# Fifty elementwise instructions go from GpSimd to VectorE between attention and the up projection

## Chip, core and metric

The kernel runs on one core of a Trainium2 chip. The metric is the device time of one execution in microseconds (us), lower is better. Before the change the median of three runs is 1442.89 us (1441.45 to 1444.49). The execution that was profiled took 1444.43 us; its trace spans 1442.6 us.

The engines are named as in the profile: PE is TensorE (matmuls), DVE is VectorE, ACT is ScalarE, POOL is GpSimd, and SP only issues DMAs here. Each engine works through its own queue strictly in order; an instruction that waits holds up all behind it.

## The reference, cut to what matters

One decoder layer on x of 1024 positions by 1024 features, all in float32:

```python
h = rmsnorm(x, attn_norm_g[l]); proj = h @ w_in[l]
# two groups of eight attention heads; each group normalised, then one output projection
x = x + o @ w_out[l]
h = rmsnorm(x, ffn_norm_g[l])
u = causal_dwconv(h @ w_up[l], conv_w[l], conv_b[l])     # width 3
gate, val = jnp.split(u, 2, axis=-1)                     # 2816 columns each
x = x + (jax.nn.silu(gate) * val) @ w_down[l]
return rmsnorm(x, final_norm_g)
```

The change touches the stretch from `o @ w_out` to the first columns of `h @ w_up`.

## The kernel before, in words

**Matmuls in two parts.** Float32 operands are split into a high part (a cast, `wh`, `xh`, ...) and a low part (the value less its high part, `wl`, `xl`, ...). `mm3` (L158 to 161) does each product in three matmuls: high by high, high by low, low by high. So each weight tile needs a cast, usually on ACT, and a subtraction, on DVE or POOL, before PE can use it. In the profile a matmul of line L161 takes a `wl` or an `xl`.

**The output projection** (loop at L772) makes x2 = x + o @ w_out in 16 products: halves c = 0, 1 of the positions, and m = 0 to 7, 128 features each. DVE takes each product out of PSUM (L790, `t`), adds it to x (L791), and SP stores it (L792). ACT squares it (L800) and a running sum `sqa` is kept (L802). The weights come in tiles `w_o` of 1024 columns, two pieces each, split by `W.split` (L131): with `act=True` the cast is on ACT (L140) and the low part on POOL (L143). Eight tiles of w_out and the first three of w_up (`w_up[0..2]`, NPRE = 3) are of this kind, 22 pieces in all. During half c = 1 DVE also normalises half 0 (`normed`, L766) and takes its low parts `b11`, `b21` (L762).

**The norm of half 1.** When the last sum of squares is there, PE adds over the features (L749), DVE and ACT make the factor `rr`, PE spreads it over partitions (L184), ACT copies it to `rbc` (L758). Then the second half can be normalised (L766; for q = 3 and 7 ACT and POOL do it, L949).

**The up projection** multiplies in a seven-product scheme (Strassen and Winograd), step j = 0 to 21, with weight blocks a11, a12, a22 and sums s1 to s4 of weight blocks, and the activations `b11, b21, b22` and their sums `t1` to `t4`. For j < 3 the products with a11 and a12 are done early (`first`, `second`), from `w_up`. The loop after L944 makes t1 to t4 and b22, all on DVE, with casts on ACT. `raws(j)` loads the two raw weight tiles of a step (v and g) into two buffers that are shared by all raw weights (`wraw`, bufs=2): a load starts when everything that reads the old tile is done. `sums` and `sums2` (L879 to 887) make s1 to s4 on POOL; s1, s2 and s3 have one buffer each, and s4 lies in that of s2. `produce` casts on ACT (L905) and takes the low part (L907): s1 and s3 on DVE, the rest on POOL. The split tiles lie in three pair buffers (`wspl`), free again when PE has used them.

**What sets the order.** SP's queue stands in program order. For the other engines a scheduler sets the order when the kernel is built, so that moving an instruction to another engine can also move its neighbours.

Of the kernel before, what the change touches and what calls it, by code (L numbers as in the profile page):

```python
# [13 lines left out]
ALU = mybir.AluOpType  # L14
# [11 lines left out]
NJ = DFF // P  # L26
# [23 lines left out]
LO_UP = ("s3", "s1")  # L50
LO_FIRST = ("a11", "a22", "a12")
# [12 lines left out]
def f32(ap):  # L64
    return ap.bitcast(F32)
# [3 lines left out]
def layer(ctx, tc, xT, wqk, wv0, wv, wout, wup, wdn, cols, fbias, yT):  # L69
    nc = tc.nc  # L70
# [43 lines left out]
    class W:  # L114
# [16 lines left out]
        def split(self, upto):  # L131
            if self.done == 0 and upto > 0:
                self.dma()
                self.hi = self.pool.tile([P, self.n if self.own else 1056], F32R, name=self.tag + "h")
                self.lo = self.pool.tile([P, self.n if self.own else 1056], F32R, name=self.tag + "l")
            while self.done < upto:
                q = self.n // self.pieces
                sl = slice(self.done * q, (self.done + 1) * q)
                if self.act:
                    nc.scalar.copy(self.hi[:, sl], self.raw[:, sl])  # L140
                else:
                    nc.gpsimd.tensor_scalar(self.hi[:, sl], self.raw[:, sl], 1.0, 0.0, ALU.mult, ALU.add)  # L142
                nc.gpsimd.tensor_tensor(self.lo[:, sl], self.raw[:, sl], f32(self.hi[:, sl]), ALU.subtract)  # L143
                self.done += 1

        def get(self):
# [78 lines left out]
    rbc = const.tile([P, T], F32, name="rbc")  # L225
# [107 lines left out]
    with tc.tile_pool(name="ps_0", bufs=6, space=PSUM) as ps0, \  # L333
            tc.tile_pool(name="st0", bufs=4) as st0:
        sqa = st0.tile([P, T], F32, name="sqa", bufs=1)
# [13 lines left out]
        for k in range(KT):  # L349
# [8 lines left out]
            else:  # L358
                sq = st0.tile([P, T], F32, name="sq", bufs=2)
# [5 lines left out]
        for k in range(KT):  # L365
# [4 lines left out]
            for u in range(2):  # L370
                wh, wl = w_qk[u].get()
                for c in range(2):
                    if k == 0:
                        psq[u, c] = ps0.tile([P, 512], F32, name="p0")
                    sl = slice(c * 512, (c + 1) * 512)
# [253 lines left out]
    def out_step(part, m, c, k, ps):  # L629
        og = fill["og"]  # L630
        sl = slice(c * 512, (c + 1) * 512)
        w = w_o[part, m // 2]
        wh, wl = w.get()
        kk = (m % 2) * 4 + k
        oh, ol = og[k if part == 0 else 4 + k]
        mm3(ps, wslice(wh, kk), wslice(wl, kk), oh[:, sl], ol[:, sl], k == 0, k == 3)
        return w, sl
# [90 lines left out]
    x2 = {}  # L728

    def load_x2(m, c):  # L730
        x2[m, c] = x2p.tile([P, 512], F32, name=f"x2_{m}_{c}")
        nc.sync.dma_start(x2[m, c], x2d[m][c])
# [6 lines left out]
    def bank():  # L739
        turn[0] += 1  # L740
        if (turn[0] - 1) % 8 < 6:
            return ps_u.tile([P, 512], F32, name="u")
        return ps_p.tile([P, 512], F32, name="pj")

    def norm_cols(sqs, n):
        pn = bank()
        for tb in range(n):
            for i, sq in enumerate(sqs):
                nc.tensor.matmul(pn[:, tb:tb + 1], sq[:, tb * P:(tb + 1) * P], ones,  # L749
                                 start=(i == 0), stop=(i == len(sqs) - 1))  # L750
        rr = small.tile([P, TB], F32, name="rr")
        rsqrt_mean(rr[:, :n], pn[:, :n], n, D)
        return rr

    def norm_rows(rr, n, dst):
        pb = bank()
        spread(pb, rr, 0, n)
        nc.scalar.copy(dst, pb[:, :n * P])  # L758
# [5 lines left out]
    def normed(k, c):  # L764
        t = x2[k, c]
        nc.vector.scalar_tensor_tensor(t, t, gcol(C_GF, k), rbc[:, c * 512:(c + 1) * 512],  # L766
                                       op0=ALU.mult, op1=ALU.mult)
        return t

    sqs = {}  # L770
    for c in range(2):
        sl = slice(c * 512, (c + 1) * 512)  # L772
        for m in range(KT):
            if (m, c) not in x2:
                load_x2(m, c)
            if c == 0:
                if m + 4 < KT and (m + 4, 0) not in x2:
                    load_x2(m + 4, 0)
                if m >= 4:
                    for q in (2 * m - 8, 2 * m - 7):  # L780
                        load_x2(q, 1)
            if c == 0 and m < 2:
                ps = box[m]
            else:
                ps = bank()
                for k in range(4):
                    w, _ = out_step(1 + c, m, c, k, ps)
                    w.ahead(((m % 2) * 4 + k + 1) / 8)
            t = stg.tile([P, 512], F32, name="t1", tag="full")
            nc.vector.tensor_tensor(t, ps, rbc[:, sl], ALU.mult)  # L790
            nc.vector.tensor_tensor(x2[m, c], x2[m, c], t, ALU.add)  # L791
            nc.sync.dma_start(x2f[m][c], x2[m, c])  # L792
            if m == 0:
                if c == 1:
                    rr = norm_cols(sqs[0], 4)
                sqa = x2p.tile([P, 512], F32, name="sqa")
                act(sqa, x2[m, c], AF.Square)
            else:
                sq = stg.tile([P, 512], F32, name="sq", tag="hl")
                act(sq, x2[m, c], AF.Square)  # L800
                if m < KT - 1:
                    nc.gpsimd.tensor_tensor(sqa, sqa, sq, ALU.add)  # L802
                else:
                    sqs[c] = (sqa, sq)
            if c == 1:
                if m == 1:
                    norm_rows(rr, 4, rbc[:, :512])
                elif m > 1:
                    for k in (m - 2,) if m < 6 else (2 * m - 8, 2 * m - 7):
                        f = normed(k, 0)  # L810
                        split(b11[k] if k < 4 else b21[k - 4], f)
# [60 lines left out]
    def sums(j):  # L872
        d = st[j]
        w = steps[j][2] * P
        g, v = d["g"], d["v"]
        for n in ("s1", "s2", "s3"):
            d[n] = sp_.tile([P, 512], F32, name=n)[:, :w]
        d["s4"] = d["s2"]
        nc.gpsimd.tensor_tensor(d["s1"], v[:, :w], v[:, w:], ALU.add)  # L879
        nc.gpsimd.tensor_tensor(d["s2"], d["s1"], g[:, :w], ALU.subtract)  # L880

    def sums2(j):
        d = st[j]
        w = steps[j][2] * P
        g, v = d["g"], d["v"]
        nc.gpsimd.tensor_tensor(d["s3"], g[:, :w], v[:, :w], ALU.subtract)
        nc.gpsimd.tensor_tensor(d["s4"], g[:, w:], d["s2"], ALU.subtract)

    def pair_tile():
        return wspl.tile([P, 1056], F32R, name="wh"), wspl.tile([P, 1056], F32R, name="wl")  # L890

    def produce(i):
        j, n = stream[i]
        if i % 2 == 0:
            tiles[i // 2] = pair_tile()
        h, l = tiles[i // 2]
        w = steps[j][2] * P
        o = (i % 2) * 512
        raws(j)
        d = st[j]  # L900
        if n[0] == "s" and "s1" not in d:
            sums(j)
        src = {"a11": lambda: d["g"][:, :w], "a12": lambda: d["g"][:, w:],
               "a22": lambda: d["v"][:, w:]}.get(n, lambda: d[n])()
        nc.scalar.copy(h[:, o:o + w], src)  # L905
        eng = nc.vector if j > NJ or n in (LO_UP if j < NJ else LO_FIRST) else nc.gpsimd
        eng.tensor_tensor(l[:, o:o + w], src, f32(h[:, o:o + w]), ALU.subtract)  # L907
        made[j, n] = ((h, l), o)
        if n == "s2":
            sums2(j)  # L910
        if n == ("a12" if j >= NPRE else "a22"):
            raws(j + 1)
# [22 lines left out]
    def hi(dst, src):  # L935
        nc.scalar.copy(dst[0], src)

    def lo(dst, src):
        nc.vector.tensor_tensor(dst[1], src, f32(dst[0]), ALU.subtract)
# [5 lines left out]
    for k in range(4):  # L945
        f12, f22, f11, f21 = x2[k, 1], x2[k + 4, 1], x2[k, 0], x2[k + 4, 0]
        for q in (k, k + 4):
            if q in (3, 7):
                nc.gpsimd.tensor_tensor(x2[q, 1], x2[q, 1], rbc[:, 512:], ALU.mult)  # L949
            else:  # L950
                normed(q, 1)
        nc.vector.tensor_tensor(f11, f12, f11, ALU.subtract)
        if k:
            lo(t2[k - 1], x4[k - 1])
        if k == 2:
            x4[k] = x2p.tile([P, 512], F32, name="sqa")
        else:
            x4[k] = stg.tile([P, 512], F32, name="t2f", tag="full")
        nc.vector.tensor_tensor(x4[k], f22, f11, ALU.subtract)
        hi(t2[k], x4[k])  # L960
        nc.vector.tensor_tensor(f21, x4[k], f21, ALU.subtract)
        if k < 2:
            ahead_to(k)
        if k:
            hi(t4[k - 1], x2[k + 3, 0])
# [76 lines left out]
    for j in range(NJ):  # L1042
        d = st[j]
        for n in PORD:
# [3 lines left out]
            w, o = made[j, n]  # L1048
# [59 lines left out]
    for s in range(NJ, NS):  # L1108
        c, mp, kn = steps[s]
        ev, od_ = 2 * mp, 2 * mp + 1  # L1110
        for n in PORD:
# [5 lines left out]
            w, o = made[s, n]  # L1117
# [64 lines left out]
    for i, (t0, tn) in enumerate(PARTS):  # L1182
        h, o = t0 // 512, t0 % 512
        sqa = sp_.tile([P, 512], F32, name=f"s{i % 2 + 1}")[:, :tn]
        for m in range(KT):
# [7 lines left out]
            v = y[m, h][:, o:o + tn]  # L1193
            tt(v, ps, v, ALU.add)
            sq = stg.tile([P, T], F32, name="sq", tag="hl")[:, :tn]
# [82 lines left out]
```

## Time and profile before

| | |
|---|---|
| median of three runs | 1442.89 us |
| profiled execution, its trace's span | 1444.43 us, 1442.6 us |
| busy: PE, DVE, ACT, POOL | 1315.3, 1115.6, 620.7, 859.2 us |
| instructions: DVE, POOL | 1588, 730 |

Times in the trace are us from the start of the span. Attention ends at about 660; the output projection's halves run from 662.7 and 685; the MLP's own first operands are made from 729.6; step 1 of the up projection starts on PE at 777.5, and from 832 PE has no gap until the down projection. A granted clock of 1.00 is 2.4 GHz, 0.5 is 1.2 GHz.

In the timelines a row of several instructions (x4) gives the first start and the time up to the last end.

### The profile page before, as it was taken

How to read it: one execution, taken by the hardware profiler on the slowest of the kernel's cores; microseconds unless marked ns; L12 is line 12 of the kernel's file. 1: busy time of each engine (PE TensorE's matmuls, PEld its weight loads, DVE VectorE, ACT ScalarE, POOL GpSimd, SP SyncE). 2: the span in 40 equal slices, each digit the busy share in tenths (PEclk: the TensorE clock that was granted, in tenths of full speed). 3: DMA queues.
4: the chain of work that ended last, by engine and by line, in shares of the span. 5: the costliest groups of instructions: out<-in, count | busy, mean ns of one | idle time of the engine just before them, and what ended most of it. 6: DMA issues, size and time to landing. Idle time of an engine off the chain costs nothing.

```text
span 1442.6 us, 19157 instructions
## 1 busy us (share of the span) xinstructions
PE 1315.3 (91%) x6640; PEld 1076.8 (75%) x6640; DVE 1115.6 (77%) x1588; ACT 620.7 (43%) x1128; POOL 859.2 (60%) x730
## 2 busy tenths in 40 slices
PE   7999999999898887889788899999999988999895
PEld 5879877877787765677556688888888866878685
DVE  6246555655676677787979999998888999899987
ACT  5134434445454564353443443344334454344334
POOL 7344454444747573454657788887877774455423
PEclk9999999999999999899979999999999999999998
DMA  5556555545444455547321233333222265544313
GB/s 179 180 160 181 152 158 158 153 142 131 153 116 122 118 170 139 167 140 259 120 80 59 81 110 109 110 109 110 95 96 95 85 222 201 176 156 146 113 35 117
DMA packets 97233, 194.89 MB, mean 135 GB/s; under 512 B 8680, under 2 KB 35688, under 8 KB 97136
## 3 DMA queue, kind: packets, MB, share of 16 engines
q1 hardware_dynamic: 96272, 193.04, 42.7%
q8 instruction: 52, 0.85, 0.2%
q10 hardware_dynamic: 864, 0.64, 0.1%
q14 instruction: 45, 0.37, 0.1%
HBM read 132.79 MB, written 60.85 MB: 134 GB/s over the span
## 4 chain that ended last, share of the span: by engine, by line
PE 50%; DMA 16%; DVE 14%; POOL 9%; issue 7%; ACT 2%; SPq 2%; DVEq 0%; POOLq 0%; ACTq 0%
PE u L161 8%; PE u L160 8%; PE u L159 8%; PE pj L161 5%; PE pj L159 5%; PE pj L160 5%; DVE fbt L493 3%; DMA q<-qkd 2%; DMA vd<-vs 2%; DMA wraw<-in_wqk_dram 2%; POOL wl L907 2%; DMA wraw<-in_wv_dram 2%; PE tp L505 2%; DMA fbt<-nfd 2%; PE o L526 2%
## 5 line engine op out<-in xcount | busy, mean ns | idle before, releaser
L143 POOL TENSOR_TENSOR wl<-wraw,wh 128x256 fp32r<-128x256 f32 (+2 forms) x134 | 124.5, 947 | 29.0 <-ACT wh L140 28.7
L494 POOL TENSOR_TENSOR w<-w,fbt 128x128 f32<-128x128 f32 (+3 forms) x64 | 90.5, 1423 | 85.5 <-DVE fbt L493 56.3
L905 ACT CAST wh<-s 128x512 fp32r<-128x512 f32 (+1 forms) x136 | 79.9, 591 | 128.3 <-POOL s L880 69.5
L493 DVE TENSOR_TENSOR_SCAN fbt<-fbt 128x128 f32<-128x128 f32 (+3 forms) x64 | 103.4, 1621 | 27.9 <-ACT fbt L480 24.1
L142 POOL TENSOR_SCALAR wh<-wraw 128x256 fp32r<-128x256 f32 (+1 forms) x112 | 57.0, 526 | 110.4 <-DMA wraw<-in_wqk_dram 59.8
L879 POOL TENSOR_TENSOR s<-wraw 128x512 f32<-128x512 f32 (+1 forms) x34 | 54.9, 1613 | 95.8 <-DVE wl L907 55.0
L505 PE MATMUL tp<-ident,w 128*128 128x128 f32 x576 | 92.9, 279 | 20.6 <-DVE pl L514 10.0
L159 PE MATMUL pj<-xh,wh 128*128 128x512 f32 x224 | 101.8, 455 | 5.2 <-DVE yf L293 5.2
L907 POOL TENSOR_TENSOR wl<-wraw,wh 128x512 fp32r<-128x512 f32 x60 | 103.0, 1723 | 0.6 <-ACT wh L905 0.6
L505 PEld LDWEIGHTS tp<-ident,w 128*128 128x128 f32 x576 | 69.8, 143 | 40.1 <-DVE pl L514 13.8
L907 POOL TENSOR_TENSOR wl<-s,wh 128x512 fp32r<-128x512 f32 x48 | 87.9, 1830 | 16.6 <-ACT wh L905 14.2
L514 DVE TENSOR_TENSOR pl<-tp,ph 128x512 fp32r<-128x512 f32 x96 | 64.9, 685 | 40.2 <-ACT ph L513 39.9
L161 PE MATMUL pj<-xh,wl 128*128 128x512 f32 x224 | 90.7, 405 | 0.0
L160 PE MATMUL pj<-xl,wh 128*128 128x512 f32 x224 | 90.2, 402 | 0.0
L485 ACT ACTIVATE w<-w,m 128x128 f32<-128x128 f32 (+3 forms) x64 | 49.7, 776 | 91.8 <-DVE m L475 85.9
L1004 DVE SCALAR_TENSOR_TENSOR tg<-ua,col,tg 128x1023 f32<-128x1023 f32 (+1 forms) x44 | 88.1, 2002 | 0.0
L480 ACT ACTIVATE fbt<-s 128x512 f32<-128x512 f32 (+2 forms) x96 | 47.8, 498 | 85.6 <-PE s L470 37.4
L489 POOL TENSOR_SCALAR w<-w,l 128x128 f32<-128x128 f32 (+3 forms) x64 | 47.9, 753 | 59.1 <-DVE l L488 31.0
L905 ACT CAST wh<-wraw 128x512 fp32r<-128x512 f32 (+1 forms) x96 | 55.1, 589 | 61.7 <-DMA wraw<-in_wdn_dram 25.3
L513 ACT CAST ph<-tp 128x512 fp32r<-128x512 f32 x96 | 55.7, 590 | 54.1 <-PE o L525 35.6
L1004 DVE SCALAR_TENSOR_TENSOR tv<-ub,col,tv 128x1023 f32<-128x1023 f32 (+1 forms) x44 | 74.0, 1681 | 5.8 <-ACT tv L1002 5.7
L466 PE MATMUL s<-kh,q 128*128 128x256 f32 (+2 forms) x192 | 69.6, 365 | 9.6 <-DMA kh<-qkd 8.0
(361 smaller groups left out, 4561.2 us busy)
## 6 DMA issues: line engine op xcount, KB each, us to landing
wraw<-in_wup_dram SPq DMA_DIRECT2D x47, 512.0 KB, 3.7
st<-td SPq DMA_DIRECT2D x74, 256.0 KB, 3.9
qkd<-hl SPq DMA_DIRECT2D x32, 512.0 KB, 3.2
td<-tg SPq DMA_DIRECT2D x44, 256.0 KB, 2.3
vd<-vs SPq DMA_DIRECT2D x32, 256.0 KB, 4.5
q<-qkd SPq DMA_DIRECT2D x16, 512.0 KB
kh<-qkd SPq DMA_DIRECT2D x32, 256.0 KB, 16.6
kl<-qkd SPq DMA_DIRECT2D x32, 256.0 KB, 17.4
```

The lines of the kernel that those rows point to most:

```text
L143: nc.gpsimd.tensor_tensor(self.lo[:, sl], self.raw[:, sl], f32(self.hi[:, sl]), ALU.subtract)
L159: nc.tensor.matmul(ps, ah, bh, start=start, stop=False)
L160: nc.tensor.matmul(ps, ah, bl, start=False, stop=False)
L161: nc.tensor.matmul(ps, al, bh, start=False, stop=stop)
L466: nc.tensor.matmul(s[:, :cn], qb, kh[:, c0:c0 + cn], start=True, stop=False)
L493: nc.vector.tensor_tensor_scan(qt[:, rev], qt[:, rev], qt[:, rev], 1.0, ALU.mult, ALU.bypass)
L494: nc.gpsimd.tensor_tensor(w[:, :n], w[:, :n], qt[:, T - n + 1:T + 1], ALU.mult)
L505: nc.tensor.transpose(tp[:, a * 256 + b * P:a * 256 + (b + 1) * P], ws[2 * g + b][:, kb * P:(kb + 1) * P], ident)
L514: nc.vector.tensor_tensor(pl[:, z:], tp[:, z:], f32(ph[:, z:]), ALU.subtract)
L905: nc.scalar.copy(h[:, o:o + w], src)
L907: eng.tensor_tensor(l[:, o:o + w], src, f32(h[:, o:o + w]), ALU.subtract)
L1004: nc.vector.scalar_tensor_tensor(t[:, s:], us[:, :T - s], col[:, cw + tap:cw + tap + 1], t[:, s:], op0=ALU.mult, op1=ALU.add)
```

## The change

```diff
@@ W.split @@
-                nc.gpsimd.tensor_tensor(self.lo[:, sl], self.raw[:, sl], f32(self.hi[:, sl]), ALU.subtract)
+                eng = nc.vector if self.act else nc.gpsimd
+                eng.tensor_tensor(self.lo[:, sl], self.raw[:, sl], f32(self.hi[:, sl]), ALU.subtract)
@@ output projection, c = 0, 1 @@
                 if m < KT - 1:
-                    nc.gpsimd.tensor_tensor(sqa, sqa, sq, ALU.add)
+                    nc.vector.tensor_tensor(sqa, sqa, sq, ALU.add)
@@ sums(j) @@
-        nc.gpsimd.tensor_tensor(d["s1"], v[:, :w], v[:, w:], ALU.add)
-        nc.gpsimd.tensor_tensor(d["s2"], d["s1"], g[:, :w], ALU.subtract)
+        eng = nc.vector if j < 2 else nc.gpsimd
+        eng.tensor_tensor(d["s1"], v[:, :w], v[:, w:], ALU.add)
+        eng.tensor_tensor(d["s2"], d["s1"], g[:, :w], ALU.subtract)
@@ sums2(j) @@
-        nc.gpsimd.tensor_tensor(d["s3"], g[:, :w], v[:, :w], ALU.subtract)
-        nc.gpsimd.tensor_tensor(d["s4"], g[:, w:], d["s2"], ALU.subtract)
+        eng = nc.vector if j < 2 else nc.gpsimd
+        eng.tensor_tensor(d["s3"], g[:, :w], v[:, :w], ALU.subtract)
+        eng.tensor_tensor(d["s4"], g[:, w:], d["s2"], ALU.subtract)
@@ produce(i) @@
-        eng = nc.vector if j > NJ or n in (LO_UP if j < NJ else LO_FIRST) else nc.gpsimd
+        eng = nc.vector if j < 2 or j > NJ or n in (LO_UP if j < NJ else LO_FIRST) else nc.gpsimd
@@ norm of half 1, q = 3, 7 @@
-                nc.gpsimd.tensor_tensor(x2[q, 1], x2[q, 1], rbc[:, 512:], ALU.mult)
+                nc.vector.tensor_tensor(x2[q, 1], x2[q, 1], rbc[:, 512:], ALU.mult)
```

Fifty instructions of 128 x 512 change engine: 22 low parts of weight pieces, 12 additions to `sqa`, 8 sums and 6 low parts of steps 0 and 1, and 2 multiplications. Nothing is added or left out. SP's order stays word for word. In the listings below, line numbers of the change are 1 to 3 higher.

DVE's queue in half c = 1, from the product m = 1 (`t1_7443`) to that of m = 3 (`t1_7500`); `x2_m_c` is x2. Before:

```order
L790 TENSOR_TENSOR t1_7443<-u_7428,rbc_251 128x512
L791 TENSOR_TENSOR x2_1_1_7274<-x2_1_1_7274,t1_7443 128x512
L766 SCALAR_TENSOR_TENSOR x2_0_0_7195<-x2_0_0_7195,col_76,rbc_251 128x512
L766 SCALAR_TENSOR_TENSOR x2_1_0_7197<-x2_1_0_7197,col_76,rbc_251 128x512
L766 SCALAR_TENSOR_TENSOR x2_2_0_7199<-x2_2_0_7199,col_76,rbc_251 128x512
L790 TENSOR_TENSOR t1_7475<-u_7456,rbc_251 128x512
L762 TENSOR_TENSOR b11l0_7180<-x2_0_0_7195,b11h0_7179 128x512
L791 TENSOR_TENSOR x2_2_1_7302<-x2_2_1_7302,t1_7475 128x512
L762 TENSOR_TENSOR b11l1_7182<-x2_1_0_7197,b11h1_7181 128x512
L762 TENSOR_TENSOR b11l2_7184<-x2_2_0_7199,b11h2_7183 128x512
L790 TENSOR_TENSOR t1_7500<-u_7485,rbc_251 128x512
```

And now, the same stretch:

```order
L791 TENSOR_TENSOR t1_7443<-u_7428,rbc_251 128x512
L767 SCALAR_TENSOR_TENSOR x2_0_0_7195<-x2_0_0_7195,col_76,rbc_251 128x512
L792 TENSOR_TENSOR x2_1_1_7274<-x2_1_1_7274,t1_7443 128x512
L767 SCALAR_TENSOR_TENSOR x2_1_0_7197<-x2_1_0_7197,col_76,rbc_251 128x512
L791 TENSOR_TENSOR t1_7475<-u_7456,rbc_251 128x512
L803 TENSOR_TENSOR sqa_7426<-sqa_7426,sq_7447 128x512
L144 TENSOR_TENSOR wl_7472<-wraw_7387,wh_7471 128x512
L792 TENSOR_TENSOR x2_2_1_7302<-x2_2_1_7302,t1_7475 128x512
L763 TENSOR_TENSOR b11l0_7180<-x2_0_0_7195,b11h0_7179 128x512
L144 TENSOR_TENSOR wl_7472<-wraw_7387,wh_7471 128x512
L803 TENSOR_TENSOR sqa_7426<-sqa_7426,sq_7479 128x512
L791 TENSOR_TENSOR t1_7500<-u_7485,rbc_251 128x512
```

Two additions to `sqa` and the two low parts of the weight tile for m = 4 and 5 now stand between the products; the third normalisation and two low parts of b11 have moved back.

POOL's queue around steps 0 to 2 (`s1_7804` is step 0's, `s1_7923` step 1's, `s1_8035` step 2's). Before:

```order
L143 TENSOR_TENSOR wl_7730<-wraw_7684,wh_7729 128x512 x2
L879 TENSOR_TENSOR s1_7804<-wraw_7800 128x512
L880 TENSOR_TENSOR s2_7805<-s1_7804,wraw_7802 128x512
L886 TENSOR_TENSOR s3_7806<-wraw_7802,wraw_7800 128x512
L907 TENSOR_TENSOR wl_7799<-s2_7805,wh_7798 128x512
L907 TENSOR_TENSOR wl_7799<-wraw_7800,wh_7798 128x512
L887 TENSOR_TENSOR s2_7805<-wraw_7802,s2_7805 128x512
L907 TENSOR_TENSOR wl_7905<-s2_7805,wh_7904 128x512
L879 TENSOR_TENSOR s1_7923<-wraw_7823 128x512
L907 TENSOR_TENSOR wl_7946<-wraw_7823,wh_7945 128x512
```

And now, from the last instruction of attention on:

```order
L495 TENSOR_TENSOR w_6886<-w_6886,fbt_4109 128x768
L881 TENSOR_TENSOR s1_8035<-wraw_7949 128x512
L910 TENSOR_TENSOR wl_8034<-wraw_7949,wh_8033 128x512
L889 TENSOR_TENSOR s3_8037<-wraw_7951,wraw_7949 128x512
L882 TENSOR_TENSOR s2_8036<-s1_8035,wraw_7951 128x512
L910 TENSOR_TENSOR wl_8034<-s2_8036,wh_8033 128x512
```

POOL has nothing left between attention and step 2's s1.

DVE's queue at the start of step 1. Before:

```order
L939 TENSOR_TENSOR b22l3_7666<-x2_7_1_7360,b22h3_7665 128x512
L907 TENSOR_TENSOR wl_7946<-s1_7923,wh_7945 128x512
L907 TENSOR_TENSOR wl_7989<-s3_7925,wh_7988 128x512
L1056 TENSOR_TENSOR u2_7921<-u_7908,m1s_7892 128x512
L1061 TENSOR_TENSOR u4_7966<-u_7953,u2_7921 128x512
```

And now:

```order
L942 TENSOR_TENSOR b22l3_7666<-x2_7_1_7360,b22h3_7665 128x512
L910 TENSOR_TENSOR wl_7905<-s2_7805,wh_7904 128x512
L881 TENSOR_TENSOR s1_7923<-wraw_7823 128x512
L1059 TENSOR_TENSOR u2_7921<-u_7908,m1s_7892 128x512
L882 TENSOR_TENSOR s2_7924<-s1_7923,wraw_7825 128x512
L889 TENSOR_TENSOR s3_7925<-wraw_7825,wraw_7823 128x512
L1001 TENSOR_TENSOR ua_7901<-pj_7774,m1s_7900 128x512
L910 TENSOR_TENSOR wl_7905<-s2_7924,wh_7904 128x512
L910 TENSOR_TENSOR wl_7946<-wraw_7823,wh_7945 128x512
L890 TENSOR_TENSOR s2_7924<-wraw_7825,s2_7924 128x512
L1064 TENSOR_TENSOR u4_7966<-u_7953,u2_7921 128x512
```

Step 1's sums and low parts now stand on DVE behind step 0's last operand, among the evictions of step 0's products.

## Rows read from the trace of the kernel before

**Rows 1.** The page's slices, each digit a fortieth of the span.

```profile
PE   7999999999898887889788899999999988999895
DVE  6246555655676677787979999998888999899987
```

**Rows 2.** Busy time by stretch (columns named in its first line).

```profile
core 0: us, PE busy (x) PEld busy (x) DVE busy (x) ACT busy (x) POOL busy (x), PEclk, DMA share, GB/s
662.70:689.70 27.00, 25.28 (x114) 19.81 (x115) 18.62 (x25) 10.70 (x19) 18.46 (x13) 1.00 0.92 325
689.70:721.00 31.30, 23.98 (x92) 17.65 (x90) 31.18 (x30) 13.93 (x24) 23.25 (x16) 0.91 0.30 102
721.00:729.60 8.60, 7.83 (x29) 6.92 (x30) 1.00 (x6) 2.52 (x6) 1.12 (x1) 0.53 0.44 152
729.60:776.70 47.10, 35.81 (x121) 24.91 (x119) 47.08 (x48) 19.55 (x34) 35.75 (x17) 0.86 0.14 39
...
832.00:1160.00 328.00, 328.00 (x1412) 265.85 (x1411) 296.58 (x263) 133.03 (x188) 264.25 (x163) 1.00 0.31 105
```

**Rows 3.** PE's waits, 662 to 845 (total us, times, longest).

```profile
PE pj L161 <- POOL wl L907: 5.2, 2, 3.0
PE u L749 <- POOL sqa L802: 4.7, 1, 4.7
PE u L161 <- POOL wl L143: 4.2, 4, 2.1
```

**Rows 4.** DVE by line and form, 729.6 to 776.7 (busy us, mean ns).

```profile
L939 DVE TENSOR_TENSOR t3l<-x,t3h 128x512 fp32r<-128x512 f32 x4 | 6.2, 1614 | 0.0
L939 DVE TENSOR_TENSOR t4l<-x,t4h 128x512 fp32r<-128x512 f32 x4 | 2.6, 680 | 0.0
```

**Rows 5.** The same for 689.7 to 721.

```profile
L791 DVE TENSOR_TENSOR x<-x,t 128x512 f32<-128x512 f32 x7 | 10.0, 1424 | 0.0
L790 DVE TENSOR_TENSOR t<-u,rbc 128x512 f32<-128x512 f32 x5 | 3.4, 680 | 1.2 <-PE u L161 1.2
```

**Rows 6.** DVE's timeline (start, duration, instruction, idle time before and what ended it).

```profile
719.23 1.76 DVE L791 TENSOR_TENSOR x<-x,t 128x512 f32<-128x512 f32 x1
...
729.62 3.58 DVE L766 SCALAR_TENSOR_TENSOR x<-x,col,rbc 128x512 f32<-128x512 f32 x2 [3.26 <-ACT rbc L758]
...
738.20 0.74 DVE L766 SCALAR_TENSOR_TENSOR x<-x,col,rbc 128x512 f32<-128x512 f32 x1
...
755.26 2.49 DVE L972 TENSOR_TENSOR x<-x,x 128x512 f32<-128x512 f32 x4
...
776.75 0.68 DVE L1056 TENSOR_TENSOR u<-u,m1s 128x512 f32<-128x512 f32 x1
```

**Rows 7.** POOL's timeline.

```profile
675.24 1.28 POOL L143 TENSOR_TENSOR wl<-wraw,wh 128x512 fp32r<-128x512 f32 x1 [1.66 <-ACT wh L140]
...
688.90 2.53 POOL L143 TENSOR_TENSOR wl<-wraw,wh 128x512 fp32r<-128x512 f32 x2 [3.53 <-ACT wh L140]
...
696.26 3.38 POOL L143 TENSOR_TENSOR wl<-wraw,wh 128x512 fp32r<-128x512 f32 x2 [1.80 <-ACT wh L140]
...
739.96 1.34 POOL L880 TENSOR_TENSOR s<-s,wraw 128x512 f32<-128x512 f32 x1 [2.23 <-DMA wraw<-in_wup_dram]
...
754.18 9.54 POOL L907 TENSOR_TENSOR wl<-s,wh 128x512 fp32r<-128x512 f32 x1 [4.21 <-ACT wh L905]
...
778.24 1.30 POOL L879 TENSOR_TENSOR s<-wraw 128x512 f32<-128x512 f32 x1 [3.77 <-DMA wraw<-in_wup_dram]
...
787.67 2.27 POOL L907 TENSOR_TENSOR wl<-wraw,wh 128x512 fp32r<-128x512 f32 x1
```

**Rows 8.** DVE by line and form, 662.7 to 689.7.

```profile
L791 DVE TENSOR_TENSOR x<-x,t 128x512 f32<-128x512 f32 x9 | 11.8, 1325 | 0.7 <-DMA x<-x2d 0.5
```

**Rows 9.** ACT's timeline, the copy of rbc for half 0.

```profile
690.13 0.59 ACT L758 COPY rbc<-u 128x512 f32<-128x512 f32 x1 [0.79 <-PE u L184]
```

**Rows 10.** PE's timeline, the first product of step 1.

```profile
777.48 0.50 PE L159 MATMUL u<-t2h,wh 128*128 128x512 f32 x1 [0.99 <-DVE u L1056]
```

## The prediction

> **What bounds the kernel now.** First the slices of the page [rows 1]: PE falls to 8 and 9 tenths in the middle of the span, where DVE rises to 9 and stays there. Then the stretches [rows 2]. From 832 PE is busy 328.00 of 328.00 us at full clock, 1412 matmuls, so one costs 0.232 us there, and nothing that DVE or POOL do in that stretch is seen in the time. From 689.7 to 776.7 it is otherwise: 92 + 29 + 121 = 242 matmuls would take 56.1 us and take 87.0, so PE loses 30.9 us, partly idle, partly at a clock of 0.53 to 0.91. DVE is busy 31.18 of 31.30 and 47.08 of 47.10 us in the two long stretches: it is the bound of this stage. But it is not working all that time. PE's waits name POOL first [rows 3]: 5.2 and 4.2 us for low parts of weights, 4.7 us for the sum of squares.
>
> The lines by form [rows 4, 5] show why DVE is full. The same subtraction of 128x512 takes 0.680 us for t4l and 1.614 us for t3l. What reads PSUM takes 0.680 (L790), the addition of two SBUF operands behind it 1.424 (L791). In the timeline [rows 6] four such instructions run in 2.49 us, the last lasting 0.68: a start every 0.60 us; a normalisation lasts 0.74 undisturbed, so 0.66; a disturbed addition lasts 1.76. POOL's instructions stand beside the disturbed ones, and one of POOL's took 9.54 us (at 754.18), while DVE was at its 0.60 pace, some fifteen instructions long [rows 6, 7]. So the two hold each other up, 1.1 us for DVE each time.
>
> **The change part by part.** Fifty instructions go to DVE at 0.60 each: 30 us more work for it. What it gets back, when POOL stands still from attention to step 2 (as POOL's queue now says), is the excess of the disturbed ones. From 662.7 to 689.7: 9 additions at 1.325 rather than 0.680, 5.8 us [rows 8]. From 689.7 to 721: 31.2 us for 30 instructions (22 at 0.60, 8 at 0.66: 18.5), 12.7. From 729.6: 47.1 for 48 (42 and 6: 29.2), 17.9. Together 36.4, more than 30; what counts is where each falls. The terms, each against the profiled execution:
>
> *Half c = 0, 662.7 to 689.7.* DVE has 8.4 us free here [rows 2], enough for the 14 moved instructions (8.4). PE is idle 27.00 - 25.28 = 1.7 us, and the DMAs are 0.92 busy, which stays. Bounds 0 and 1.7; I take 1.0.
>
> *Half c = 1, to the end of its last addition at 720.99* [rows 6]. DVE's queue has 39 instructions instead of 30 up to there: 6 additions to sqa and 6 low parts more, and one normalisation and two low parts of b moved behind it. 32 x 0.60 + 7 x 0.66 = 23.8; the second instruction now needs rbc, copied by 690.72 [rows 9], 0.4 us after its turn if the first starts at 689.70 as before; with 0.7 more, an estimate, for low parts that wait for a cast, 24.9. Before 31.3: gain 6.4. PE does not bind (seven products, 84 x 0.232 = 19.5). Bounds: 0, if such waits fill all that is won, and 7.5, without them.
>
> *The norm of half 1, 720.99 to 729.62.* This is a chain through ACT, PE and DVE's small instructions, 8.6 us, and DVE is busy only 1.00 of it [rows 2, 6]. It stays. The seven instructions that now stand in and around it (4.3 us) fit into DVE's idle 7.6. Bounds: 0 and 2.
>
> *The MLP's operands, 729.62 to 776.75.* 48 instructions become 56: plus step 0's four sums and three low parts, the two multiplications and step 1's s1, less two low parts that move back. 50 x 0.60 + 6 x 0.66 = 34.0. A new wait comes in: the first low part needs a pair buffer that PE frees at the end of the product of `second(0)`, 41 matmuls behind the spread in its queue, 9.5 us, and ACT's cast, 0.6; DVE gets there after 13 instructions, 8.1 us. So 2.0 us, in which the operands t2 and all behind them wait too. 36.0 against 47.1: gain 11.1, bounds 6 (the wait at 7, if PE runs at half clock) and 13.
>
> *Step 1.* Before, PE began it 0.73 us after DVE began u2 [rows 6, 10]. Now s2, s3, the eviction ua and the low part of s2 come behind u2: 5 x 0.60 = 3.0. Loss 2.3. Sum at the start of step 1: 1.0 + 6.4 + 11.1 - 2.3 = 16.2, so 777.5 becomes 761.3.
>
> *Step 2, the first on POOL.* Its tile v can be loaded only when DVE has taken the low part of a22 of step 1, 0.6 us behind, and the load takes 3.8, for which POOL stood already [rows 7]. Then five POOL instructions (s1, a low part, s3, s2, a low part) at 1.30 to 2.27 [rows 7] and a cast, 0.6: the low part is there 11.5 to 16.4 us after the start of step 1, and PE takes 60 x 0.232 = 13.9 for that step. PE waits 0 to 2.5; I take 1.2. Gain left: 15.0. From here on all engines have the work and the order they had, and the PE-bound stretch hands the gain on to the end.
>
> A POOL instruction of step 2 is the open size. POOL's op at 754.18 waited through some fifteen DVE instructions [rows 6, 7]. The Trainium skill (SBUF — State Buffer, Who interferes with whom) says that the shared port goes to whoever issues first and that the other is blocked until that one has finished. By that rule no POOL instruction of step 2 would take more than about 2 us; the row of 9.54 us differs, the measurement decides, and the first rival is priced by it.
>
> So 1444.43 - 15.0 = 1429.4 for the profiled execution. It is 1.5 us above the median of the runs, so the forecast is **1427.9**, with a range of its own of 1423 to 1433.
>
> **Rivals.** (a) *POOL is starved in step 2.* One of its low parts is held up as at 754.18, 9.54 - 1.30 = 8.2 us, and PE stands for it. For it: DVE evicts, converts and convolves without a gap there. Against: before, POOL's instructions in the same place took 1.30 and 2.27 [rows 7]. Gain 6.8: 1436; with part of it 1434 to 1440.
>
> (b) *More than forecast.* No new wait before the operands (2.0), none on POOL (1.2), the upper bounds of c = 0 and c = 1 (0.7 and 1.1), the shorter norm chain (2): 22, so 1421. For it: PE has still 30.9 - 16.2 = 14.7 us to lose. Against: everything has to go right.
>
> (c) *Slower: DVE takes over POOL's waits.* A low part of a weight waits for its cast, the cast for the load. On POOL such a wait held up nobody else; in DVE's queue the next evictions and operands stand behind it. POOL's six longest: 1.66 + 3.53 + 1.80 + 2.23 + 4.21 + 3.77 = 17.2 us [rows 7]. If DVE stands for all of them while PE, kept idle, falls to half clock twice more (29 matmuls in 8.6 us rather than 6.7 [rows 2], 1.9 each), 21.0 us are lost against 15.0 won: 1449. It decides from 15 us of such waits on. Against: 11.2 of these 17.2 us are for ACT, and ACT stood for DVE's own late results; DVE comes to its low parts later in its queue than POOL did.
>
> (d) *Slower: no relief.* If the disturbed instructions were slow for another reason, the two full stretches would get the 9 and 8 instructions more that their queues show and step 1 its 2.3 us: 17 x 0.60 + 2.3 = 12.5 us, 1455. Against: the same subtraction at 0.680 and 1.614 [rows 4]. On this the Trainium skill (Perfetto Trace Analysis, Optimizing Scalar/DVE Operations) says that work may be offloaded to GpSimd when DVE is saturated; the change does the reverse, and by that rule it is slower. The same passage warns that the two share a read port, so that moving work between them might not help; the rows fit this half.
>
> (e) *No change*: waits on loads and casts eat the gain. About 1443.
>
> That the moved instructions stay where they were is no rival: POOL's queue, as it stands, shows them gone.
>
> **How the numbers follow.** Forecast 0.64, (a) 0.14, (b) 0.08, (e) 0.06, (c) 0.06, (d) 0.02. A difference within 0.2% (2.9 us) cannot be told from none. Faster by more: forecast, (a) and (b), 0.86; the same: (e), 0.06; slower: 0.08. The range from 1420 to 1439 leaves out (c), (d), (e), about 0.04 of (b) and 0.02 of (a): 0.20.
>
> **What would show it.** Right: no POOL instruction between 650 and the middle of the 760s; L792 (before L791) and the low parts of t3 and b22 at 0.68; the last addition of c = 1 near 714; the first normalisation of half 1 near 722; step 1 on PE near 761; PE still without a gap from some 15 us earlier than 832. Wrong: the additions still above 1 us with POOL idle (d); DVE idle in front of low parts of weights for more than 5 us in sum (c); a POOL instruction of over 4 us in step 2 and PE waiting for it (a); a gain at step 1 that the down projection does not show.

## The result and the profile after

The changed kernel takes 1426.55 us, the median of four runs (1422.27 to 1431.94), beside 1443.69 for the kernel before (1441.45 to 1445.52); the ratio is 0.9884, interval 0.9847 to 0.9921. Timed once more, beside other kernels, it took 1425.48, ratio 0.9872 (0.9856 to 0.9889). The forecast was 1427.9, range 1420 to 1439.

The profiled execution has a span of 1430.2 us, 12.4 shorter than before. It understates the gain: the half c = 0 of the transition begins at 665.10 in it, 2.4 us later than before, and the code up to there is nearly the same. In the nine profiles below of kernels that leave the attention alone this point lies between 657.70 and 664.56, in the changed kernel's second profile at 662.62. So lengths are taken from there. To the end of the span it is 1442.6 - 662.71 = 779.9 us before, 1430.2 - 665.10 = 765.1 after, and 1425.6 - 662.62 = 763.0 in the second profile: 14.8 and 16.9 us.

First the stretches of the changed kernel, cut at the same events as those of before, to be laid beside [rows 2] (half c = 0; half c = 1 to its last addition; the norm; the MLP's operands; a stretch in which PE is never idle):

```profile
core 0: us, PE busy (x) PEld busy (x) DVE busy (x) ACT busy (x) POOL busy (x), PEclk, DMA share, GB/s
665.10:691.50 26.40, 25.88 (x119) 20.58 (x120) 20.73 (x38) 10.85 (x20) 0.00 (x0) 1.00 0.92 318
691.50:715.50 24.00, 20.14 (x87) 15.77 (x85) 24.00 (x41) 12.72 (x23) 0.00 (x0) 0.97 0.41 132
715.50:724.30 8.80, 7.16 (x26) 6.30 (x27) 5.20 (x15) 4.22 (x9) 0.00 (x0) 0.50 0.54 164
724.30:758.90 34.60, 29.31 (x106) 20.66 (x105) 34.13 (x56) 16.69 (x29) 0.00 (x0) 0.90 0.12 42
...
819.00:1146.00 327.00, 327.00 (x1407) 264.97 (x1406) 293.69 (x261) 132.07 (x185) 262.52 (x161) 1.00 0.31 105
```

The second line has 41 instructions of DVE in 24.00 us, where before it was 30 in 31.30; the fourth 56 in 34.60, where it was 48 in 47.10. DVE is as full as it was: each instruction is shorter. In the last line PE is without a gap from 819 on, 13 us before 832.

By line and form, for 665.1 to 691.5, then 691.5 to 715.5, then 724.3 to 758.9; these answer [rows 8], [rows 5] and [rows 4]:

```profile
L792 DVE TENSOR_TENSOR x<-x,t 128x512 f32<-128x512 f32 x9 | 6.1, 685 | 0.0
```

```profile
L792 DVE TENSOR_TENSOR x<-x,t 128x512 f32<-128x512 f32 x7 | 4.8, 684 | 0.0
L803 DVE TENSOR_TENSOR sqa<-sqa,sq 128x512 f32<-128x512 f32 x6 | 4.1, 684 | 0.0
```

```profile
L942 DVE TENSOR_TENSOR t4l<-x,t4h 128x512 fp32r<-128x512 f32 x4 | 2.6, 684 | 0.0
L942 DVE TENSOR_TENSOR t3l<-x,t3h 128x512 fp32r<-128x512 f32 x4 | 2.5, 683 | 0.0
```

The addition went from 1325 (c = 0) and 1424 (c = 1) to 685 and 684 ns, t3l from 1614 to 683; the moved addition to sqa costs the same. DVE's timeline, for [rows 6]:

```profile
714.82 0.69 DVE L792 TENSOR_TENSOR x<-x,t 128x512 f32<-128x512 f32 x1
...
724.30 1.42 DVE L767 SCALAR_TENSOR_TENSOR x<-x,col,rbc 128x512 f32<-128x512 f32 x2 [1.97 <-ACT rbc L759]
...
732.93 0.69 DVE L910 TENSOR_TENSOR wl<-s,wh 128x512 fp32r<-128x512 f32 x1 [0.47 <-ACT wh L908]
...
758.94 0.68 DVE L1059 TENSOR_TENSOR u<-u,m1s 128x512 f32<-128x512 f32 x1
```

POOL's timeline, for [rows 7], its last product of the attention and its next instructions, all of step 2:

```profile
640.24 2.42 POOL L495 TENSOR_TENSOR w<-w,fbt 128x768 f32<-128x768 f32 x1 [1.78 <-DVE fbt L494]
766.61 1.30 POOL L881 TENSOR_TENSOR s<-wraw 128x512 f32<-128x512 f32 x1 [123.96 <-DMA wraw<-in_wup_dram]
767.87 1.76 POOL L910 TENSOR_TENSOR wl<-wraw,wh 128x512 fp32r<-128x512 f32 x1
769.58 2.29 POOL L889 TENSOR_TENSOR s<-wraw 128x512 f32<-128x512 f32 x1
771.82 2.28 POOL L882 TENSOR_TENSOR s<-s,wraw 128x512 f32<-128x512 f32 x1
774.84 1.48 POOL L910 TENSOR_TENSOR wl<-s,wh 128x512 fp32r<-128x512 f32 x1 [0.73 <-ACT wh L908]
```

It stands for 123.96 us, and none of step 2's takes above 2.29. PE's first product of step 1, for [rows 10], and the place in step 2 where it waits for POOL:

```profile
761.13 0.50 PE L160 MATMUL u<-t2h,wh 128*128 128x512 f32 x1
...
776.37 0.50 PE L162 MATMUL u<-t2h,wl 128*128 128x512 f32 x1 [0.84 <-POOL wl L910]
```

PE's waits from 665 to 845 (total us, times, longest), for [rows 3]:

```profile
PE u L162 <- DVE wl L910: 3.0, 3, 1.9
PE u L750 <- ACT sq L801: 2.8, 1, 2.8
...
PE pj L162 <- POOL wl L910: 2.2, 1, 2.2
```

Of the waits for POOL in [rows 3], the 4.7 and 4.2 us are gone, and 3.0 of the 5.2. For the sums of squares PE now waits 1.8 us for DVE, and 2.8 for ACT where it was 1.3. The other part of the 5.2 us is still there. It is PE's last gap before the down projection in both kernels, in the fifth up step; here it is before, then now:

```profile
827.80 0.63 PE L161 MATMUL pj<-b11h,wl 128*128 128x512 f32 x1 [2.23 <-POOL wl L907]
```

```profile
813.95 0.80 PE L162 MATMUL pj<-b11h,wl 128*128 128x512 f32 x1 [2.21 <-POOL wl L910]
```

Behind it the clock is at half for a while (a mean of 0.82 from 811 to 830).

### The profile page after: what moved, and what is told of

Its sections match the earlier page's. It is cut to its first block, busy times and chain, and to the rows that moved or that the text cites. A ratio compares the mean times of both kernels' runs of the same rounds, so it can differ in the third digit from the quotient of the medians.

```text
span 1430.2 us, 19128 instructions
## 1 busy us (share of the span) xinstructions
PE 1310.7 (92%) x6640; PEld 1075.8 (75%) x6640; DVE 1111.7 (78%) x1638; ACT 620.7 (43%) x1128; POOL 773.8 (54%) x680
## 4 chain that ended last, share of the span: by engine, by line
PE 49%; DVE 18%; DMA 17%; POOL 6%; issue 5%; ACT 2%; SPq 2%; DVEq 0%; POOLq 0%; ACTq 0%
PE u L161 7%; PE u L162 7%; PE u L160 7%; PE pj L160 5%; PE pj L162 5%; PE pj L161 5%; DMA q<-qkd 4%; DVE fbt L494 3%; DMA vd<-vs 3%; DMA st<-td 2%; PE tp L506 2%; PE o L527 2%; DVE wl L910 2%; DMA wraw<-in_wv_dram 2%; PE o L526 1%
## 5 line engine op out<-in xcount | busy, mean ns | idle before, releaser
L495 POOL TENSOR_TENSOR w<-w,fbt 128x128 f32<-128x128 f32 (+3 forms) x64 | 91.2, 1434 | 90.9 <-DVE fbt L494 59.8
L494 DVE TENSOR_TENSOR_SCAN fbt<-fbt 128x128 f32<-128x128 f32 (+3 forms) x64 | 102.9, 1616 | 27.9 <-ACT fbt L481 24.2
L910 POOL TENSOR_TENSOR wl<-wraw,wh 128x512 fp32r<-128x512 f32 x58 | 100.0, 1730 | 0.0
L144 POOL TENSOR_TENSOR wl<-wraw,wh 128x256 fp32r<-128x256 f32 (+1 forms) x112 | 89.1, 814 | 0.3
L278 PE MATMUL pj<-wh,xh 128*128 128x256 f32 (+1 forms) x256 | 78.5, 307 | 0.8 <-DVE yf L294 0.8
L910 POOL TENSOR_TENSOR wl<-s,wh 128x512 fp32r<-128x512 f32 x44 | 73.4, 1668 | 9.4 <-ACT wh L908 9.2
```

The source lines that it names most:

```text
L144: eng.tensor_tensor(self.lo[:, sl], self.raw[:, sl], f32(self.hi[:, sl]), ALU.subtract)
L278: nc.tensor.matmul(ps[:, :n], xh[k][:, sl], h, start=(k == 0), stop=False)
L494: nc.vector.tensor_tensor_scan(qt[:, rev], qt[:, rev], qt[:, rev], 1.0, ALU.mult, ALU.bypass)
L495: nc.gpsimd.tensor_tensor(w[:, :n], w[:, :n], qt[:, T - n + 1:T + 1], ALU.mult)
```

## The experiments

The theory: a DVE instruction with two operands in SBUF and a GpSimd instruction that reads SBUF hold each other up, and the change wins because GpSimd stands still. The main rival: GpSimd's results simply came late, and DVE is quicker at making them.

**One part at a time.** The first has the weights' low parts and the sums of squares on DVE, nothing else:

```
-nc.gpsimd.tensor_tensor(self.lo[:, sl], self.raw[:, sl], f32(self.hi[:, sl]), ALU.subtract)
+eng = nc.vector if self.act else nc.gpsimd
+eng.tensor_tensor(self.lo[:, sl], self.raw[:, sl], f32(self.hi[:, sl]), ALU.subtract)
...
-nc.gpsimd.tensor_tensor(sqa, sqa, sq, ALU.add)
+nc.vector.tensor_tensor(sqa, sqa, sq, ALU.add)
```

> Only the low parts of the output projection's weights and the sums of squares go to the vector engine; the sums, the low parts of steps 0 and 1 and the two multiplications stay on GpSimd. Theory of mutual hold-up: the additions (t added to x2) of both halves last 0.68 us, the last addition of half c = 1 comes 6 to 8 us earlier, and from the first normalisation of half 1 to the start of step 1 all stays as slow as before (47 us of DVE, t3l at about 1.6 us). The end gains about 7 us: 1436, ratio 0.995. Rival, that GpSimd's lateness alone was the trouble (its results came late and DVE is merely quicker at them): the additions stay above 1.2 us since DVE has more to do, and the gain is under 3 us: 1441 or more.

The second has the rest of the diff, without these edits:

> Only the four sums and the low parts of steps 0 and 1 and the two multiplications by rbc go to the vector engine; the low parts of the output projection's weights and the sums of squares stay on GpSimd. Theory of mutual hold-up: the additions stay at 1.3 to 1.4 us up to the end of half c = 1 (no gain there), the low parts of t3 and b22 last 0.68 us, and the stretch from the first normalisation of half 1 to the start of step 1 is 9 to 13 us shorter. The end gains 8 to 11 us: 1434, ratio 0.993. The two parts together should give the whole change, 17 us. Rival, lateness alone: the low parts of t3 stay near 1.6 us, and 12 more instructions on DVE make it 3 us slower or no faster: 1443 to 1446.

Measured: 1433.89, ratio 0.9935 (0.9910 to 0.9959), and 1436.23, ratio 0.9948 (0.9932 to 0.9965). The parts' gains, 6.5 and 5.2 thousandths, add up to the whole's 11.6 (12.8 when timed again). In the first kernel's lines by form from 662 to 725 the additions are quick, and t3l in its timeline is still slow, 5.15 us for four:

```profile
L792 DVE TENSOR_TENSOR x<-x,t 128x512 f32<-128x512 f32 x16 | 10.9, 689 | 0.0
```

```profile
751.28 5.15 DVE L940 TENSOR_TENSOR t3l<-x,t3h 128x512 fp32r<-128x512 f32 x4
```

In the second kernel the same two views read the other way round:

```profile
L791 DVE TENSOR_TENSOR x<-x,t 128x512 f32<-128x512 f32 x16 | 21.2, 1330 | 0.7 <-DMA x<-x2d 0.4
```

```profile
757.15 2.49 DVE L941 TENSOR_TENSOR t3l<-x,t3h 128x512 fp32r<-128x512 f32 x4
```

Where GpSimd was silenced these instructions fell below 0.70 us each; where it was not they stayed slow. The first part won 3 us more than expected: from the first normalisation of half 1 to step 1 it took 45.0 us (719.56 to 764.57) where it was 47.9 before. The second, with 7.7 us, just missed its 8 to 11.

**GpSimd busy again, with work that nobody waits for (e3_pool_reads).** To the changed kernel 48 instructions on GpSimd are added. PE, DVE, ACT and the DMA queue keep the order that they had. In the transition two stand behind each addition to x2 (one behind the last), and 17 behind the second norm:

```
+def idle_pool(s, n): [nc.gpsimd.tensor_tensor(stp.tile([P, 512], F32, name="st"), s, s, ALU.add) for _ in range(n)]
...
-nc.sync.dma_start(x2f[m][c], x2[m, c])
+nc.sync.dma_start(x2f[m][c], x2[m, c]); idle_pool(x2[m, c], 2 if c == 0 or m < 7 else 1)
...
-x4 = {}
+x4 = idle_pool(rbc[:, 512:], 17) or {}
```

> The changed kernel, with 48 additions of 128x512 put on GpSimd that nobody reads or waits for: 31 in the transition, each reading a finished tile of x2 from SBUF twice, and 17 that read rbc behind the second norm. Theory of mutual hold-up: DVE's instructions with two SBUF operands last 1.3 to 1.7 us again while these run, the 32 of half c = 1 and the first normalisations lose about 15 us, the MLP's operands about 15: 1450 to 1460, slower than the kernel before. Rival, lateness alone: nothing waits for them, so 1427 and L792 at 0.68 us.

Measured: 1452.71, ratio 1.0071 (1.0044 to 1.0098), slower than before; lateness alone is refuted. None of DVE's waits from 655 to 800 is for GpSimd: its instructions last longer, they do not wait for results. GpSimd's timeline shows the 17 as one row:

```profile
733.96 24.18 POOL L770 TENSOR_TENSOR st<-rbc 128x512 f32<-128x512 f32 x17 [7.22 <-ACT rbc L759]
```

DVE's timeline at the same time, with the end of that stretch:

```profile
736.91 1.52 DVE L955 TENSOR_TENSOR x<-x,x 128x512 f32<-128x512 f32 x1
738.36 1.52 DVE L881 TENSOR_TENSOR s<-wraw 128x512 f32<-128x512 f32 x1
739.81 1.52 DVE L962 TENSOR_TENSOR t2f<-x,x 128x512 f32<-128x512 f32 x1
...
757.16 1.52 DVE L910 TENSOR_TENSOR wl<-wraw,wh 128x512 fp32r<-128x512 f32 x1
758.61 1.40 DVE L767 SCALAR_TENSOR_TENSOR x<-x,col,rbc 128x512 f32<-128x512 f32 x2
759.93 0.68 DVE L955 TENSOR_TENSOR x<-x,x 128x512 f32<-128x512 f32 x1
760.53 0.68 DVE L942 TENSOR_TENSOR t2l<-t2f,t2h 128x512 fp32r<-128x512 f32 x1
```

The two take turns, one for one: DVE starts every 1.45 us, GpSimd every 24.18 / 17 = 1.42. When GpSimd has done its 17, DVE is back at a start every 0.60.

**Reading or writing (e4_pool_writes, e5_pool_single).** In place of each addition two fills of 128x512 with zero; one read of a single column starts each group:

```
+def idle_pool(s, n): t = stp.tile([P, 512], F32, name="st"); nc.gpsimd.tensor_scalar(t[:, :1], s[:, :1], 1.0, 0.0, ALU.mult, ALU.add); [nc.gpsimd.memset(t, 0.0) for _ in range(2 * n)]
```

> The changed kernel, with 96 fills of 128x512 with zero put on GpSimd at the places of the additions of the other experiment (two fills in place of each addition, and one read of a single column in front of each group so that they start there): GpSimd is busy and writes SBUF, but reads next to nothing. If it is GpSimd's reading that holds DVE up (the Trainium skill, SBUF - State Buffer, says that a DVE instruction with two SBUF inputs is blocked only by a GpSimd instruction that reads SBUF), L792 lasts 0.68 us and the time stays at 1427, within 3 us. Rival: any GpSimd work beside DVE does it, by writing too, and the additions are above 1 us: 1440 to 1460.

And the additions replaced by an instruction that reads its tile once:

```
+def idle_pool(s, n): [nc.gpsimd.tensor_scalar(stp.tile([P, 512], F32, name="st"), s, 1.0, 0.0, ALU.mult, ALU.add) for _ in range(n)]
```

> The changed kernel with 48 GpSimd instructions that nobody waits for, at the places of the additions of e3_pool_reads, but each reads one SBUF tile of 128x512 once (tensor_scalar, times 1 plus 0) instead of twice. In e3 DVE and GpSimd took turns, one for one, at 1.45 us. Theory A, any reading by GpSimd holds DVE up (so the Trainium skill, SBUF - State Buffer, has it): they take turns again, at 0.6 us more the duration of the GpSimd instruction, about 0.5 us, so 1.1; 32 turns of 0.5 us lost, 1440. Theory B, only GpSimd's second input collides with DVE's second input: L792 at 0.68 us and 1426.

The fills: 1429.03, ratio 0.9902 (0.9880 to 0.9925), which meets both intervals of the changed kernel. Its lines by form, DVE from 662 to 725 and GpSimd from 640 to 790:

```profile
L792 DVE TENSOR_TENSOR x<-x,t 128x512 f32<-128x512 f32 x16 | 11.0, 693 | 0.0
```

```profile
L770 POOL MEMSET st<- 128x512 f32 x96 | 50.2, 526 | 5.1
```

The fills keep GpSimd busy for 50.2 us; 62 of the 96 belong to the two halves, where DVE's additions stay at 693 ns. The single reads: 1439.19, ratio 0.9965 (0.9952 to 0.9978), as theory A had it. DVE beside them, and GpSimd's row:

```profile
731.58 1.09 DVE L962 TENSOR_TENSOR t2f<-x,x 128x512 f32<-128x512 f32 x1
732.59 1.09 DVE L767 SCALAR_TENSOR_TENSOR x<-x,col,rbc 128x512 f32<-128x512 f32 x1
733.61 1.10 DVE L964 TENSOR_TENSOR x<-t2f,x 128x512 f32<-128x512 f32 x1
```

```profile
727.89 17.47 POOL L770 TENSOR_SCALAR st<-rbc 128x512 f32<-128x512 f32 x17 [6.57 <-ACT rbc L759]
```

A turn takes 1.02 us. So both kinds of reading that were tried cost DVE, 0.42 us with one operand and 0.85 with two. The Trainium skill (SBUF — State Buffer, Who interferes with whom) says so: a DVE instruction with two SBUF inputs contends with GpSimd instructions that read, not with those that only write. These runs agree. Its other sentence, that the loser is blocked for the whole of the other's instruction, does not fit to the number: GpSimd's addition lasts 1.30 undisturbed [rows 7], and DVE lost 0.85 beside it. In the kernel before, a disturbed DVE instruction lost up to 1.1 (1.76 against 0.68 [rows 4, 6]); why more than beside the added reads was not tried.

**How far it carries.** Three kernels extend the change, timed beside the unedited one. In j3 the bound is step 3, in jall NJ, all up steps; in jfull these lines are always nc.vector, and so is what GpSimd does in operands(), combine() and plain_split():

```
-eng = nc.vector if j < 2 else nc.gpsimd
+eng = nc.vector if j < 3 else nc.gpsimd
```

> The changed kernel once more, unedited, beside the next three on one chip, since its ratio so far goes from 0.985 to 0.992. Theory of mutual hold-up: the sum of the two parts, 0.9935 and 0.9948, so 0.988: 1427.

> Step 2 too has its sums and low parts on the vector engine (j < 3 in place of j < 2). GpSimd then begins with step 3. Theory of mutual hold-up: DVE's convolution beside step 2 lasts 1.28 us an instruction and not 2.31, which pays for the seven more instructions, and PE's wait of 0.84 us for a low part of step 2 goes: 1 us faster than the change to 1 us slower, 1426. Rival, that any more work on DVE is now too much, since it is busy 54.4 of 55.1 us there: 3 to 5 us slower than the change, 1430.

> All up steps have their sums and low parts on the vector engine. By the trace of the changed kernel, from 819 to 1146 DVE's instructions beside GpSimd take about 81 us more than undisturbed ones (convolution 1.28, product with tv 1.23, combinations 0.68), and GpSimd runs 161: 0.50 us for each, less than the 0.60 us that one costs on DVE. Theory of mutual hold-up: DVE's busy share there goes from 0.90 to about 0.95, PE stays the bound, the end within 3 us of the change: 1427. Rival, that work taken from GpSimd always pays (the relief of 0.7 us for an instruction, as in the transition): DVE's share falls below 0.88. Rival, no relief in this stretch: DVE would need 390 us for 327 and the end comes 60 us later.

> As the one before, and the sums, low parts and operands of the down projection as well: GpSimd stands still from the transition to the last rows. In the down projection DVE binds (143.6 of 154 us busy) and PE waits some 13 us for its low parts, while GpSimd runs 53 instructions there. Theory of mutual hold-up, with the relief of 0.5 us of the up steps against costs of 0.50 to 0.60 us: within 5 us of the change either way, 1429. Rival, a relief of 0.7 us or more: 5 to 10 us faster, 1419. Rival, no relief: 53 x 0.55 = 29 us slower, 1456.

Measured: the change 1425.48, ratio 0.9872; j3 1427.62, 0.9883 (0.9860 to 0.9905), no difference; jall 1421.29, 0.9834 (0.9818 to 0.9851); jfull 1418.66, 0.9815 (0.9792 to 0.9839). The last two beat both kernels; their intervals overlap, so which is best stays open. The stretch from 819 to 1140, of the changed kernel in its second profile, then of jall:

```profile
819.00:1140.00 321.00, 321.00 (x1383) 260.16 (x1382) 290.65 (x257) 128.57 (x180) 259.85 (x158) 1.00 0.31 104
```

```profile
819.00:1140.00 321.00, 321.00 (x1382) 259.87 (x1381) 308.99 (x413) 132.04 (x182) 13.61 (x9) 1.00 0.32 105
```

156 more instructions cost DVE 18.3 us: 0.12 each, so 0.48 of the 0.60 comes back, as worked out (0.50). PE is the bound in both. The time fell 4.2 us, 1 more than expected: PE's waits for POOL's low parts of up weights, 2.2 and 0.8 us, are gone, and its listed waits from 755 on sum to 24.2 us, where they were 27.0. Where the rest lies was not settled. In jfull the window from 1140 to 1300, mostly down projection, has 241 instructions on DVE where the change has 187, and they keep it busy 146.57 us and not 149.48: there the relief is more than the cost. The relief of 0.5 us, on which the forecast of 1429 rests, was too low for that stretch; the time is that of the rival with 0.7 or more.

**Where it ends.** Two kernels go on from jfull into the attention, f1_attn_mult with the first edit, f2_attn_low with the second:

```
-nc.gpsimd.tensor_tensor(w[:, :n], w[:, :n], qt[:, T - n + 1:T + 1], ALU.mult)
+nc.vector.tensor_tensor(w[:, :n], w[:, :n], qt[:, T - n + 1:T + 1], ALU.mult)
...
-eng = nc.vector if self.act else nc.gpsimd
+eng = nc.vector
```

> The kernel jfull with one thing more: in the attention the product of the stick-breaking weights (L495, 64 instructions, 91 us on GpSimd, for which PE waits 8.4 us in all) on the vector engine. There DVE mostly reads PSUM with its first input and is 0.46 to 0.69 busy, so little is held up and little is to be won back: some 49 us of work for it, hidden in its idle time. Theory: PE's waits for L495 shrink to a few us, 1 to 5 us faster than jfull, 1416. Rival, DVE's queue is in the way (its product stands behind other work, the deferred results come later): 2 to 10 us slower than jfull, 1424.

> The kernel jfull with the low parts of all other weights of the projections (112 instructions of 128x256, 0.8 us each on GpSimd) on the vector engine as well, some 40 us of work. DVE's instructions beside them read PSUM and last 0.68 us, undisturbed, so by the theory of mutual hold-up nothing is to be won back, PE's one wait for such a low part is 1.6 us, and DVE's idle time hides the work: within 3 us of jfull, 1419. Rival, that work taken from GpSimd pays everywhere: 10 us or more faster, 1409. Rival, DVE's queue is in the way: 1425 or more.

Measured: 1432.41, ratio 0.9934 (0.9910 to 0.9957), by the medians 14 us slower than jfull, which was timed on another occasion; and 1461.42, ratio 1.0118 (1.0095 to 1.0141), 43 us slower. Both forecasts failed, in the direction of the rival that has DVE's queue in the way; for the first that rival, with 2 to 10 us, was too small as well. The half c = 0 begins at 670.45 and 700.66 in the profiles, in jfull's at 664.56. The spans are 4.8 and 37.4 us longer than jfull's, so nearly all of this lies before the transition. In the second, DVE's own waits up to 700 (total us, times, longest), then PE's up to 660:

```profile
DVE wl L144 <- POOL wh L142: 60.5, 18, 10.1
```

```profile
PE o L527 <- DVE pl L515: 42.7, 10, 8.3
PE tp L506 <- DVE pl L515: 20.3, 10, 9.5
```

The low part waits in DVE's queue for the cast, which GpSimd still makes from a load, and the attention's low parts pl stand behind it: PE waits 63 us for them, where in jfull it waits 21.6 (12.2 and 9.4). This is rival (c) of the prediction, in a place where the cast is not early. In the first, DVE is busy 84.61 of the 100 us from 400 on, where it was 69.66 in jfull, and PE's waits for pl and ptl (29.2 us up to 660, 25.9 in jfull) did not shrink, while the 6.9 us for L495 went. These do not account for 14 us; the cause stays open.

## Why the prediction was right, point by point

*What bounds the kernel, and the relief.* Right. The lockstep of 1.45 us against 0.60, the single reads in between and the fills without effect show the mechanism that the prediction had inferred from two durations of one subtraction. Rival (d), no relief, is refuted: with GpSimd silent the additions and t3l, slow before, last 0.68.

*The terms*, each measured from the stretch's own start, forecast in brackets. Half c = 0: 691.55 - 665.10 = 26.5 against 27.0, gain 0.5 (1.0). Half c = 1: 24.0 against 31.3, gain 7.3 (6.4); the 0.7 put in for waits on casts did not show there, DVE was busy 24.00 of 24.00. The norm: 8.8 against 8.6, loss 0.2 (0). The MLP's operands: 724.30 to 758.94, 34.6 against 47.1, gain 12.5 (11.1); the wait for the pair buffer was 0.47, not 2.0. Step 1: PE began 2.2 us behind u2's start, against 0.7, loss 1.5 (2.3). Sum 18.6, where 16.2 was forecast. By absolute times the 2.4 us by which this execution began the stage later hide the difference: step 1 at 761.13, forecast 761.3. But the two starts of step 1 are not the same place in PE's work. Before, PE had done all 12 matmuls of step 1's product with t4 by then; now the scheduler has put 10 of them behind. The rows show a matmul of this product, before and now:

```profile
768.14 0.63 PE L159 MATMUL pj<-t4h,wh 128*128 128x512 f32 x1
...
777.48 0.50 PE L159 MATMUL u<-t2h,wh 128*128 128x512 f32 x1 [0.99 <-DVE u L1056]
```

```profile
761.13 0.50 PE L160 MATMUL u<-t2h,wh 128*128 128x512 f32 x1
...
764.84 0.39 PE L162 MATMUL pj<-t4h,wl 128*128 128x512 f32 x1
```

These 10 at 0.232 are 2.3 us, so the stage gained 16.3. That this is the forecast 16.2 is luck: terms set 2.4 us too low and an order of PE's queue that was taken as kept cancel.

*Step 2, and what is given back.* PE waited 0.84 for POOL there (1.2). The prediction then handed the gain on unchanged, and it was so up to PE's last gap: from the start of c = 0 to there it took 165.1 us before, 148.9 now and 148.7 in the second profile, a gain of 16.2 and 16.4. PE's waits from step 1 up to there and at it sum to 4.2 us in both kernels: 0.48, 1.36, 0.15 and 2.23 before, 0.84, 0.89, 0.25 and 2.21 now. At the end 14.8 us remain in this profile and 16.9 in the second. Behind the gap the clock differs: in the next 17 us it was 0.90 with 67 matmuls before, 0.82 with 61 now, 0.92 with 68 in the second profile. Six matmuls at 0.232 are 1.4 us, what this profile gives back. The runs gained 17.1 us, and 18.9 when timed again, beside 15.0 forecast.

*The mis-sized terms*: chiefly the wait of 2.0 us for the pair buffer and the 0.7 for casts in c = 1, together 2.2 us of the 2.4. They were estimates of new waits, each set too high. What the prediction put at nothing is PE's order at step 1, the 2.3 us above.

*The rivals.* (a) did not happen: no POOL instruction of step 2 above 2.29. (c): DVE's waits for casts before low parts were 1.2 and 0.5 us from 665 to 765, far below the 15 from which it decides (its "six longest" waits are those for casts and loads; one for rbc, 7.55 us at 729.67, was longer); the attention kernel shows what it would have looked like. (b), more than forecast, came true in a part: nearly no new wait before the operands. (e) did not happen: the gain is far over 2.9 us.

*The Trainium skill's advice* (Perfetto Trace Analysis, Optimizing Scalar/DVE Operations) to offload a saturated DVE to GpSimd: here DVE was saturated, and the reverse paid, as the second half of that passage allows.

## What to carry to other kernels

Before GpSimd is given work beside a full DVE, compare the same DVE instruction with and without GpSimd at its side. Where DVE read two SBUF operands here, each GpSimd instruction of 128x512 that read SBUF took 0.4 to 1.1 us of it, so elementwise work of 0.60 us nearly or more than paid for its own move; fills took nothing. In the attention, where DVE mostly reads PSUM, both moves lost. Where the moved instruction must wait for a result of GpSimd itself, leave it there: DVE's queue then stalls for everything behind it.

## What was not expected of the hardware

The turns are exact: 17 GpSimd additions go with 17 DVE instructions of about 1.52 us, and 17 single reads with 17 of about 1.09. Yet in the kernel before one GpSimd instruction stood 9.54 us while DVE ran at its pace of 0.60 [rows 6, 7]. The traces give a hint. That instruction ended 1.23 us, about one addition, behind the start of DVE's next instruction that reads PSUM (L942, `hold`, at 762.49). The fills' kernel shows the same: its one-column reads by GpSimd, 0.19 us undisturbed, took up to 2.62, and the three longest each ended 0.14 or 0.15 us behind the start of a DVE instruction that reads PSUM. GpSimd's row and DVE's:

```profile
709.42 2.62 POOL L770 TENSOR_SCALAR st<-x 128x1 f32<-128x1 f32 x1
```

```profile
711.89 0.71 DVE L791 TENSOR_TENSOR t<-pj,rbc 128x512 f32<-128x512 f32 x1
```

So in these cases a GpSimd read that came while DVE ran two-operand SBUF work without a pause stood until DVE did something else. That is not the whole rule, since elsewhere the two take turns; what decides between the two was not tried.
